# Nine gate/up pairs of the feed-forwards from three narrow matmuls per block to a wide and a narrow one

## The chip, the cores and the metric

The kernel runs on one core of a Trainium2 chip. The metric is the time of one execution on the device, in microseconds (us), as the median of several runs. Besides, one execution was recorded by the hardware profiler; its views (the page, groups of instructions, waits, the timeline) are quoted below. The engines are TensorE (PE; its weight loads are PEld), VectorE (DVE), ScalarE (ACT), GpSimd (POOL) and SyncE (SP), which issues the loads.

## The reference

One decoder layer on 512 tokens of width 1024: a feed-forward, a mixer (attention beside a recurrence), and a second feed-forward. Only the feed-forwards matter here, each of width 2816:

```
f = (silu(x @ w_gate) * (x @ w_up)) @ w_down
h = h + 0.5 * rms_norm(f, g)
```

Everything is float32.

## The kernel before, in words

**Two parts for each number.** TensorE multiplies a shortened float32. To keep the precision, each operand is split into a high part (the value rounded to the short form) and a low part (what is left). `split` does it: a copy on ScalarE writes the high part (L302), a subtraction on VectorE the low part (L303). A product then takes three matmuls for each block of 128 rows: high weights with the high input, high weights with the low input, low weights with the high input, all added up in one accumulator in PSUM.

**Seven products for eight.** The width 2816 is 22 tiles of 128 columns, numbered f = 0 to 21. The first few tiles of each feed-forward (six and three) are plain products. For each later tile the gate and the up projection are computed together as a *pair*: the contraction of 1024 is cut into two halves and the tokens into two halves of 256, and the 2 x 2 blocks of gate and up are obtained from seven products of sums of blocks (p1 to p7) instead of eight. `w_forms` makes the sums of the weights on VectorE and splits them; the sums of the input are made once. Each product runs over four row tiles of 128 (called blocks here), so a pair in the narrow form is 7 x 4 x 3 = 84 matmuls of 256 columns. The results come from chains: p1 is copied to a second accumulator, p6 and p7 go on adding to the first, and so on.

**The narrow form.** `seven_on` (L733) uses four accumulators of 256 columns. It runs p1, p5, p6, p2, p7, p3, p4 through `seventh` (L729 to L731 are its three matmuls). Between them ScalarE copies an accumulator to another or to SBUF (L743), always with higher priority. The gate's first half goes through Silu straight out of PSUM (L958), VectorE adds the second halves (L944 for the gate, which then goes through Silu at L945, L949 for up), and L954 multiplies gate and up, in two halves.

**The wide form.** `seven_wide` (L762) is in the kernel already, for the 16 pairs of the mixer. Its accumulators are whole PSUM banks of 512 columns, five of them. For each block one matmul of 512 columns (L779) multiplies the high weights with the high and the low input side by side, and one of 256 columns (L780) adds the low weights' product to the second half. So the two halves of a bank must be added when the chain ends: `fold` copies one half on ScalarE (L790) and adds the other on VectorE (L791); `sum_of` needs two adds on VectorE (L797, L798). `move` copies a bank of 512 columns to the next accumulator on ScalarE (L784).

**The down projection.** It is done in parts of four tiles, again by seven products, in four steps per part that are laid between the pairs: `ffn_order` writes the order of the events (weights of the next pair, weights of a down step, pair, down step) and `STEPS_AT` says which step follows which pair. In a step `down7` runs two or four groups of six matmuls of 512 columns (L1037 to L1039). Before a group, ScalarE writes the sum so far into its accumulator (the seed, L1026); after it, ScalarE copies it out (L1042). There are three such accumulators (`aux`), so the fourth group's seed waits for the first group's copy. `d_forms` makes the weights of a step. The tiles of the last part (f from 16 on) are split and wait for `last_product`, the plain product that ends a feed-forward.

**What sets the order.** Each engine runs its instructions in the order in which a scheduler has put them when the program is built; it goes by the order of the code and by priorities (`tc.high_priority`: weights ahead by 100, evictions of a pair by 200). Buffers come from pools: five accumulators `acc`, three `aux`, four weight tiles `w8` (1024 columns, both parts) and two `w4`, four raw weight buffers. So a weight tile for the next pair can only be split once an older one has been used, and a raw one can only be loaded once it has been split.

**At the pairs.** `prod` (L937) computes tile f. As `FIRST_ON` is 5, the narrow `seven_on` serves f = 6 to 21 of the first feed-forward and f = 5 to 21 of the second; f = 3 and 4 of the second use an older form, `seven`.

Of the kernel before, what the change touches and what calls it, by code (L numbers as in the profile page):

```python
# [20 lines left out]
NF = 22  # L21
FF_PARTS = ((0, 4), (4, 8), (8, 12), (12, 16), (16, 22))
NSTD = {1: 6, 2: 3}

SEVEN = range(4)
STEPS_AT = {1: ((6, 7, 7, 8), range(9, 13), range(13, 17), range(17, 21)),
# [4 lines left out]
HB = 256  # L31
# [3 lines left out]
FIRST_ON = {1: 5, 2: 5}  # L35
# [30 lines left out]
def ffn_order(n):  # L66

    order = [("std", f) for f in range(NSTD[n])]  # L70
    after = {}
# [3 lines left out]
    ready = False  # L75
    for f in range(NSTD[n], NF):
        if not ready:
# [106 lines left out]
def hybrid_layer(ctx: ExitStack, tc: tile.TileContext, xT: bass.AP, xN: bass.AP, wst: bass.AP,  # L184
# [120 lines left out]
    def acc_ps():  # L305
        return psum.tile([P, T], F32, name="acc", tag="acc", bufs=5)
# [4 lines left out]
    def tmp(name):  # L311
        return tpool.tile([P, T], F32, name=name, tag="t")
# [39 lines left out]
    HALVES = (slice(0, HB), slice(HB, T))  # L352
# [369 lines left out]
    def seventh(t, w, p, ps, start):  # L722
        at = t[p].at
        if len(at(0, 0).shape) == 3:
            ps = ps.rearrange("q (b t) -> q b t", b=2)
        for k in range(4):
            ks = slice(k * P, (k + 1) * P)
            wh, wl, xh, xl = w[p][:, 0, ks], w[p][:, 1, ks], at(0, k), at(1, k)
            PE.matmul(ps, wh, xh, start=start and k == 0, stop=False, skip_group_check=True)  # L729
            PE.matmul(ps, wh, xl, start=False, stop=False, skip_group_check=True)  # L730
            PE.matmul(ps, wl, xh, start=False, stop=k == 3, skip_group_check=True)  # L731

    def seven_on(t, w, g0, g1, u0, u1):  # L733

        b, z, y, v = (acc_ps()[:, :HB] for _ in range(4))

        def copy(ps, dst=None):
            if dst is None:  # L740
                dst = tpool.tile([P, HB], F32, name="c", tag="c", bufs=CB)
            with tc.high_priority(offset=EVAC):
                ACT.activation(dst, ps, AF.Copy)  # L743
            return dst

        seventh(t, w, "p1", b, True)
        copy(b, y)
        seventh(t, w, "p5", z, True)
        c5 = copy(z)
        seventh(t, w, "p6", b, False)  # L750
        c6 = copy(b)
        seventh(t, w, "p2", y, False)
        g0(y)
        seventh(t, w, "p7", b, False)
        copy(b, v)
        u1(b, c5)
        seventh(t, w, "p3", z, False)
        g1(z, c6)
        seventh(t, w, "p4", v, False)
        u0(v)  # L760

    def seven_wide(t, w, g, u, seen=lambda ap: ap, then=lambda: None):  # L762


        b, z, y, v, o = (acc_ps() for _ in range(5))

        def two(ps):
            return ps[:, :HB], ps[:, HB:]

        def product(p, ps, start):  # L770
            at = t[p].at
            part, cross = ps.rearrange("q (s c) -> q s c", s=2), two(ps)[1]
            if len(at(0, 0).shape) == 3:
                part = ps.rearrange("q (s b t) -> q s b t", s=2, b=2)
                cross = cross.rearrange("q (b t) -> q b t", b=2)
            for k in range(4):
                ks = slice(k * P, (k + 1) * P)
                wh, wl = w[p][:, 0, ks], w[p][:, 1, ks]
                PE.matmul(part, wh, at(BOTH, k), start=start and k == 0, stop=False, skip_group_check=True)  # L779
                PE.matmul(cross, wl, at(0, k), start=False, stop=k == 3, skip_group_check=True)  # L780

        def move(dst, src):
            with tc.high_priority(offset=EVAC):
                return ACT.activation(dst, src, AF.Copy).ins  # L784

        def fold(ps, dst=None):
            out = tpool.tile([P, HB], F32, name="c", tag="c", bufs=CB) if dst is None else dst
            x, y_ = two(ps) if dst is None else map(seen, two(ps))
            with tc.high_priority(offset=EVAC):
                ACT.activation(out, x, AF.Copy)  # L790
                DVE.tensor_add(out, y_, out)  # L791
            return out

        def sum_of(dst, ps, c):
            x, y_ = two(ps)
            with tc.high_priority(offset=EVAC):
                DVE.tensor_add(c, x, c)  # L797
                DVE.tensor_add(dst, seen(y_), seen(c))  # L798

        product("p1", b, True)  # L800
        move(y, b)
        product("p5", z, True)
        c5 = fold(z)
        product("p6", y, False)
        move(v, y)
        c6 = fold(y)
        product("p2", b, False)
        fold(b, g[0])
        product("p7", v, False)
        moved = move(o, v)  # L810
        sum_of(u[1], v, c5)
        with tc.issue_after(moved):
            then()
        product("p3", z, False)
        sum_of(g[1], z, c6)
        product("p4", o, False)
        fold(o, u[0])

    def seven(t, w, z, g, u):


        b, y = acc_ps()[:, :HB], acc_ps()[:, :HB]

        def product(p, ps, start):
            seventh(t, w, p, ps, start)

        def copy(ps):
            c = tpool.tile([P, HB], F32, name="c", tag="c", bufs=CB)
            with tc.high_priority(offset=EVAC):
                ACT.activation(c, ps, AF.Copy)  # L830
            return c

        def sum_of(dst, ps, c):
            with tc.high_priority(offset=EVAC):
                DVE.tensor_add(dst, ps, c)

        product("p1", b, True)
        c1 = copy(b)
        product("p2", y, True)
        sum_of(g[0], y, c1)  # L840
        product("p6", b, False)
        c6 = copy(b)
        product("p5", z, True)
        c5 = copy(z)
        product("p7", b, False)
        c7 = copy(b)
        sum_of(u[1], c7, c5)
        product("p4", y, True)
        sum_of(u[0], y, c7)
        product("p3", z, False)  # L850
        sum_of(g[1], z, c6)

    def ffn(n, x, r, forms_x, apool, pss):
        t, steps = forms_x
# [81 lines left out]

        def prod(f, w):  # L937
            g, u = tmp("g"), tmp("u")
            if f >= FIRST_ON[n]:
                lo, hi = HALVES  # L940

                def g1(z, c6):
                    with tc.high_priority(offset=EVAC):
                        DVE.tensor_add(g[:, hi], z, c6)  # L944
                    ACT.activation(g[:, hi], g[:, hi], AF.Silu)  # L945

                def u1(b, c5):
                    with tc.high_priority(offset=EVAC):
                        DVE.tensor_add(u[:, hi], b, c5)  # L949

                def u0(v):
                    def put(dst, view):
                        for q, (h, src) in enumerate(zip(HALVES, (v, u[:, hi]))):
                            DVE.scalar_tensor_tensor(dst[:, q] if len(dst.shape) == 3 else dst[:, h], g[:, h], -1.0,  # L954
                                                     src, op0=ALU.mult, op1=ALU.mult)
                    into(f, put)

                seven_on(t, w, lambda y: ACT.activation(g[:, lo], y, AF.Silu), g1, u0, u1)  # L958
                return
            seven(t, w, acc_ps()[:, :HB], [g[:, h] for h in HALVES], [u[:, h] for h in HALVES])  # L960
            ACT.activation(g, g, AF.Silu)
            into(f, lambda dst, v: DVE.scalar_tensor_tensor(dst, v(g), -1.0, v(u), op0=ALU.mult, op1=ALU.mult))

# [96 lines left out]

        keys = [(w, n, i) for i in range(NSTD[n]) for w in ("gate", "up")]
        forms = {}
        for ev in ffn_order(n):
            if ev[0] == "std":
                j = ev[1]
                while len(pss) < 2 * j + 2:
                    pss.append(acc_ps())
                    gemm(pss[-1], fetch(keys[len(pss) - 1]), x)
                with tc.high_priority(offset=EVAC if j == NSTD[n] - 1 else 0):
                    std_out(pss[2 * j], pss[2 * j + 1], j)  # L1070

                for step in steps[j:] if j == min(NSTD[n], 4) - 1 else steps[j:j + 1]:
                    step()
# [123 lines left out]
    with ExitStack() as mx:  # L1197
# [38 lines left out]
        def values_two(steps, then):  # L1236
# [78 lines left out]
            for j in range(2):  # L1315
# [4 lines left out]
        t, steps = forms_of(lambda i, j: Form(lambda s, k: um_t[2 * i + k // 2][:, s, k % 2, HALVES[j]]),  # L1320
                            apool, False, rec_half)
# [167 lines left out]
        for c in range(0, KC, 2):  # L1489
            g, u = tmp("g"), tmp("u")  # L1490
# [12 lines left out]
    with ExitStack() as mx:  # L1503
# [146 lines left out]
        for i, (what, hd) in enumerate(LRU_ORDER):  # L1650
# [9 lines left out]
            def then():  # L1660
                if i + 1 < len(LRU_ORDER):
                    prepare(LRU_ORDER[i + 1])
# [21 lines left out]
        for c in range(KC):  # L1684
            if c < 3:
                ps = pss[c]
            else:
# [17 lines left out]
                 {(1, 3): lambda: (bd2.turn(0), bd2.turn(1))})  # L1705
    keys = [(w, 2, i) for i in range(NSTD[2]) for w in ("gate", "up")]
    pss = gemm_first(keys[:NFIRST], u2, [spare(ap2)["tx"]],
# [144 lines left out]
```

## Time and profile before

| | |
|---|---|
| median of 3 runs | 1212.2 us (1211.42 to 1212.27) |
| the profiled execution | 1211.87 us |
| its span, first to last instruction | 1210.1 us |
| first feed-forward's pairs, f = 6 to 21 | about 72 to 310 us |
| mixer's wide pairs | about 407 to 600 us |
| second feed-forward's pairs, f = 3 to 21 | about 900 to 1171 us |

In a row of the groups stand line, engine, operation, tile written and tiles read, shape and count, then the busy time in us and the mean of one in ns, then the idle time of the engine just before them and what ended it. In a timeline row stand the start and the duration in us. A row of the waits names who waited for whom, with total us, times and longest. A row of the stretches gives the length, and the busy time of each engine asked for, in the order PE, PEld, DVE, ACT, POOL, then the granted clock.

### The profile page before, as it was taken

What the parts mean: (1) busy time and instruction counts of PE and PEld (TensorE: products, weight loads), DVE (VectorE), ACT (ScalarE), POOL (GpSimd) and SP (SyncE); (2) the same over time, 40 slices, a digit from 0 to 9 for tenths busy, and PEclk for the clock granted to TensorE, in tenths of its full rate; (3) what the DMA queues carried; (4) which work ended last, traced back from release to release, by engine and by line L of the source; (5) the groups of instructions that cost most, each with busy time, mean ns of one, the idle gap of its engine ahead of it and who ended that gap; (6) DMA issues with size and microseconds to landing.
All of it is one profiled execution on the core that took longest, in us unless ns stands there. A gap on an engine that the chain in (4) does not pass through costs nothing.

```text
span 1210.1 us, 18990 instructions
## 1 busy us (share of the span) xinstructions
PE 1199.2 (99%) x7306; PEld 1073.7 (89%) x7306; DVE 1029.0 (85%) x1608; ACT 832.4 (69%) x1447; POOL 26.1 (2%) x51
## 2 busy tenths in 40 slices
PE   9999999999999999999999999999999999999997
PEld 8899999999888889888889888888899999999996
DVE  7999888989689899999867899775799888888964
ACT  7566787887566576677735897834566687877763
POOL 0000000000011000000000000000100000000000
PEclk9999999999999999999999999999999999999999
DMA  7234343435625232222323432235443333343341
GB/s 266 87 97 140 114 138 116 133 118 157 243 109 145 70 114 79 88 96 70 126 77 111 145 135 87 87 110 186 148 137 117 123 121 125 121 130 115 123 174 70
DMA packets 45819, 149.78 MB, mean 124 GB/s; under 512 B 5152, under 2 KB 8608, under 8 KB 45728
## 3 DMA queue, kind: packets, MB, share of 16 engines
q1 hardware_dynamic: 38160, 131.09, 32.5%
q0 software_dynamic: 7280, 17.30, 4.2%
q8 instruction: 57, 0.93, 0.3%
q14 instruction: 34, 0.28, 0.1%
q10 hardware_dynamic: 288, 0.17, 0.0%
HBM read 138.06 MB, written 6.29 MB: 119 GB/s over the span
## 4 chain that ended last, share of the span: by engine, by line
PE 88%; DVE 6%; ACT 3%; DMA 2%; issue 1%; DVEq 0%
PE acc L729 9%; PE acc L731 9%; PE acc L730 9%; PE acc L779 8%; PE acc L315 7%; PE acc L317 7%; PE acc L316 7%; PE acc L780 4%; PE aux L1037 3%; PE aux L1038 3%; PE aux L1039 3%; DVE w L303 2%; DMA raw<-in_w 2%; PE acc L433 2%; PE acc L432 2%; PE acc L431 2%
## 5 line engine op out<-in xcount | busy, mean ns | idle before, releaser
L303 DVE TENSOR_TENSOR w<-raw,w 128x1024 fp32r<-128x1024 f32 (+1 forms) x272 | 297.4, 1098 | 36.2 <-ACT w L302 35.2
L302 ACT ACTIVATE w<-raw 128x1024 fp32r<-128x1024 f32 (+1 forms) x272 | 259.9, 959 | 89.4 <-PE acc L317 42.7
L729 PE MATMUL acc<-big,w 128*128 128x256 f32 x920 | 260.5, 283 | 0.0
L731 PE MATMUL acc<-big,w 128*128 128x256 f32 x920 | 260.3, 283 | 0.0
L730 PE MATMUL acc<-big,w 128*128 128x256 f32 x920 | 260.3, 283 | 0.0
L729 PEld LDWEIGHTS acc<-big,w 128*128 128x128 f32 x920 | 176.2, 192 | 1.9
L730 PEld LDWEIGHTS acc<-big,w 128*128 128x128 f32 x920 | 176.2, 192 | 1.7
L731 PEld LDWEIGHTS acc<-big,w 128*128 128x128 f32 x920 | 176.3, 192 | 0.0
L779 PE MATMUL acc<-big,w 128*128 128x512 f32 x320 | 115.0, 397 | 0.0
L780 PE MATMUL acc<-big,w 128*128 128x256 f32 x320 | 90.8, 284 | 0.0
L1037 PE MATMUL aux<-w,xf 128*128 128x512 f32 x224 | 87.5, 393 | 1.4 <-ACT w L302 0.9
L1038 PE MATMUL aux<-w,xf 128*128 128x512 f32 x224 | 87.5, 391 | 0.0
L1039 PE MATMUL aux<-w,xf 128*128 128x512 f32 x224 | 87.2, 389 | 0.0
L779 PEld LDWEIGHTS acc<-big,w 128*128 128x128 f32 x320 | 60.1, 188 | 13.2 <-ACT acc L784 0.2
L303 DVE TENSOR_TENSOR w<-s,w 128x1024 fp32r<-128x1024 f32 x51 | 62.2, 1220 | 3.2 <-ACT w L302 2.7
L780 PEld LDWEIGHTS acc<-big,w 128*128 128x128 f32 x320 | 60.4, 189 | 0.1
L315 PE MATMUL acc<-xf,w 128*128 128x512 f32 (+1 forms) x168 | 58.8, 352 | 0.0
L316 PE MATMUL acc<-xf,w 128*128 128x512 f32 (+1 forms) x168 | 58.6, 349 | 0.0
L317 PE MATMUL acc<-xf,w 128*128 128x512 f32 (+1 forms) x168 | 58.6, 349 | 0.0
L302 ACT ACTIVATE w<-s 128x1024 fp32r<-128x1024 f32 x51 | 53.9, 1057 | 6.2 <-PE acc L731 3.0
L743 ACT ACTIVATE c<-acc 128x256 f32<-128x256 f32 x74 | 28.2, 383 | 40.4 <-PE acc L731 40.2
L1037 PEld LDWEIGHTS aux<-w,xf 128*128 128x128 f32 x224 | 41.9, 188 | 10.2 <-ACT w L302 1.5
(453 smaller groups left out, 2934.2 us busy)
## 6 DMA issues: line engine op xcount, KB each, us to landing
raw<-in_w SPq DMA_DIRECT2D x232, 512.0 KB, 3.5
big<-xf POOLq DMA_DIRECT2D x6, 512.0 KB, 3.4
gains<-in_rows POOLq DMA_DIRECT2D x5, 512.0 KB, 5.4
h<-in_x SPq DMA_DIRECT2D x8, 256.0 KB, 5.3
h<-in_xn POOLq DMA_DIRECT2D x4, 512.0 KB, 6.0
kept_m<-h POOLq DMA_DIRECT2D x4, 512.0 KB, 2.9
vals<-in_w SPq DMA_DIRECT2D x4, 512.0 KB, 6.2
h<-kept_m POOLq DMA_DIRECT2D x4, 512.0 KB, 6.1
```

The lines of the kernel that those rows point to most:

```text
L302: state["split"] = ACT.activation(dh, src, AF.Copy).ins
L303: state["low"] = DVE.tensor_sub(dl, src, dh.bitcast(F32)).ins
L315: PE.matmul(ps, wh, xh, start=first, stop=False)
L316: PE.matmul(ps, wh, xl, start=False, stop=False)
L317: PE.matmul(ps, wl, xh, start=False, stop=last)
L729: PE.matmul(ps, wh, xh, start=start and k == 0, stop=False, skip_group_check=True)
L730: PE.matmul(ps, wh, xl, start=False, stop=False, skip_group_check=True)
L731: PE.matmul(ps, wl, xh, start=False, stop=k == 3, skip_group_check=True)
L779: PE.matmul(part, wh, at(BOTH, k), start=start and k == 0, stop=False, skip_group_check=True)
L780: PE.matmul(cross, wl, at(0, k), start=False, stop=k == 3, skip_group_check=True)
L1037: PE.matmul(ps, xh, wh, start=first and j == 0, stop=False, skip_group_check=True)
L1038: PE.matmul(ps, xh, wl, start=False, stop=False, skip_group_check=True)
```

## The change

A table names nine tiles, four of the first feed-forward and five of the second, and `prod` hands these to `seven_wide` instead of `seven_on`. Gate and up come out as whole tiles in SBUF, so the code behind the branch, which until now served only the older form, does the Silu over 512 columns and one product over 512 columns. The computation is the same. In the first feed-forward the tiles 10, 14 and 18 have a down step of four groups behind them, and so have 9, 13 and 17 in the second; behind tile 20 of the second comes tile 21, and behind tile 21 of either the last product.

```diff
+WIDE = {1: (10, 14, 18, 21), 2: (9, 13, 17, 20, 21)}
...
         def prod(f, w):
             g, u = tmp("g"), tmp("u")
-            if f >= FIRST_ON[n]:
+            if f in WIDE[n]:
+                seven_wide(t, w, *([x[:, h] for h in HALVES] for x in (g, u)))
+            elif f >= FIRST_ON[n]:
                 lo, hi = HALVES
...
                 seven_on(t, w, lambda y: ACT.activation(g[:, lo], y, AF.Silu), g1, u0, u1)
                 return
-            seven(t, w, acc_ps()[:, :HB], [g[:, h] for h in HALVES], [u[:, h] for h in HALVES])
+            else:
+                seven(t, w, acc_ps()[:, :HB], [g[:, h] for h in HALVES], [u[:, h] for h in HALVES])
             ACT.activation(g, g, AF.Silu)
             into(f, lambda dst, v: DVE.scalar_tensor_tensor(dst, v(g), -1.0, v(u), op0=ALU.mult, op1=ALU.mult))
```

The function that is now called, cut to its core:

```python
def seven_wide(t, w, g, u, seen=lambda ap: ap, then=lambda: None):
    b, z, y, v, o = (acc_ps() for _ in range(5))
...
        for k in range(4):
...
            PE.matmul(part, wh, at(BOTH, k), start=start and k == 0, stop=False, skip_group_check=True)
            PE.matmul(cross, wl, at(0, k), start=False, stop=k == 3, skip_group_check=True)
...
    product("p1", b, True)
    move(y, b)
    product("p5", z, True)
    c5 = fold(z)
    product("p6", y, False)
    move(v, y)
    c6 = fold(y)
    product("p2", b, False)
    fold(b, g[0])
    product("p7", v, False)
    moved = move(o, v)
    sum_of(u[1], v, c5)
...
    product("p3", z, False)
    sum_of(g[1], z, c6)
    product("p4", o, False)
    fold(o, u[0])
```

All line numbers are those of the kernel before, as in its profile.

## The prediction

> **What bounds the kernel now.** The page comes first: its busy table says which engine fills the span, its slices whether the clock was granted, and its groups what a matmul costs in either form.
>
> ```profile
> span 1210.1 us, 18990 instructions
> ...
> PE 1199.2 (99%) x7306; PEld 1073.7 (89%) x7306; DVE 1029.0 (85%) x1608; ACT 832.4 (69%) x1447; POOL 26.1 (2%) x51
> ...
> PEclk9999999999999999999999999999999999999999
> ```
>
> TensorE is busy 99% of 1210.1 us at full clock; VectorE (85%) and ScalarE (69%) are behind it. So time falls only where TensorE's own stream gets shorter, and rises where another engine makes it wait. The waits of TensorE in the second feed-forward (895 to 1192 us) show how little waiting there is to win:
>
> ```profile
> PE aux L1037 <- ACT w L302: 0.9, 3, 0.5
> PE aux L1037 <- ACT aux L1026: 0.5, 1, 0.5
> ```
>
> In the first one (60 to 320 us) this view has no row at all: the 16 pairs and their down steps there run without a gap.
>
> A matmul's duration in the groups overlaps the next one's, so I read prices from starts. The timeline of TensorE, from the first matmul of one pair to the first of what follows: narrow pair 10 of the first feed-forward, then three stretches of 28 wide blocks of the mixer (one block is the matmuls of one of the four row tiles of a product) that ran without a wait.
>
> ```profile
> 136.73 0.28 PE L729 MATMUL acc<-big,w 128*128 128x256 f32 x1
> ...
> 146.81 0.40 PE L1037 MATMUL aux<-w,xf 128*128 128x512 f32 x1
> ...
> 407.01 0.39 PE L779 MATMUL acc<-big,w 128*128 128x512 f32 x1
> ...
> 416.89 0.39 PE L779 MATMUL acc<-big,w 128*128 128x512 f32 x1
> ...
> 455.08 0.39 PE L779 MATMUL acc<-big,w 128*128 128x512 f32 x1
> ...
> 464.86 0.39 PE L779 MATMUL acc<-big,w 128*128 128x512 f32 x1
> ...
> 489.15 0.39 PE L779 MATMUL acc<-big,w 128*128 128x512 f32 x1
> ...
> 498.89 0.39 PE L779 MATMUL acc<-big,w 128*128 128x512 f32 x1
> ```
>
> Narrow: 146.81 - 136.73 = 10.08 us for 84 matmuls, 0.36 per block of three. Wide: 9.88, 9.78 and 9.74 us for 56 matmuls, 0.353 to 0.348 per block of two. Both forms stream the same 768 columns per block; a pair differs by 0.20 to 0.34 us, not by a third.
>
> **The change, part by part.** *The pace.* At nine pairs 84 matmuls become 56 (-252 in all). Saving between 9 x 0.20 = 1.8 and 9 x 0.34 = 3.1 us. I take the middle one of the three stretches, 0.30 a pair, 2.7 us.
>
> [...]
>
> *The evictions.* Prices from the mixer, where the wide form runs already (405 to 602 us), beside the narrow form's (60 to 320 us):
>
> ```profile
> L784 ACT ACTIVATE acc<-acc 128x512 f32<-128x512 f32 x48 | 28.3, 589 | 11.0 <-PE acc L780 8.4 <-DVE e L1437 1.1 <-DVE xch L1415 1.1
> L790 ACT ACTIVATE c<-acc 128x256 f32<-128x256 f32 x32 | 12.1, 379 | 9.1 <-PE acc L780 8.9
> L791 DVE TENSOR_TENSOR c<-acc,c 128x256 f32<-128x256 f32 x32 | 13.4, 420 | 4.0 <-ACT c L790 3.9
> L743 ACT ACTIVATE c<-acc 128x256 f32<-128x256 f32 x32 | 12.1, 382 | 14.2 <-PE acc L731 14.1
> L949 DVE TENSOR_TENSOR u<-acc,c 128x256 f32<-128x256 f32 x16 | 6.7, 418 | 0.0
> L303 DVE TENSOR_TENSOR xf<-tt,xf 128x512 fp32r<-128x512 f32 x12 | 8.1, 686 | 0.0
> ```
>
> A pair on ScalarE: four copies and two half Silus (6 x 0.38 = 2.3 us) become three moves of 0.59, four copies of 0.38 and one Silu of 512 columns (about 0.6, as the move): 3.9 us, so +1.6. On VectorE: two adds and two half products (4 x 0.42 = 1.7) become eight adds of 0.42 and one product of 512 columns (0.69, as the last row): 4.1 us, so +2.4. Whether that is hidden is read from busy times of the stretches of pair 10 with its down step, and of pair 20 of the second feed-forward, which has no down step behind it:
>
> ```profile
> 136.73:152.27 15.54, 15.54 (x109) 1.00 0.39 123
> ...
> 136.70:152.20 15.50, 15.50 (x109) 14.54 (x108) 12.53 (x17) 12.01 (x23) 0.00 (x0) 1.00 0.38 121
> ...
> 1150.50:1160.60 10.10, 10.10 (x86) 10.06 (x85) 8.06 (x11) 7.62 (x15) 0.00 (x0) 1.00 0.43 144
> ```
>
> Pair 10: VectorE (third busy time) has 3.0 us idle, ScalarE (fourth) 3.5; both additions fit. Pair 20: VectorE has 2.0 idle against 2.4, short by 0.4. What covers that is the lead of the weights: the low half for product p5 of pair 11 is split at 148.21 and used at 153.71.
>
> ```profile
> 148.21 1.23 DVE L303 TENSOR_TENSOR w<-s,w 128x1024 fp32r<-128x1024 f32 x1 [0.17 <-ACT w L302]
> ...
> 153.71 0.28 PE L729 MATMUL acc<-big,w 128*128 128x256 f32 x1
> ```
>
> That is 153.71 - 149.44 = 4.3 us of cover. So I cost both additions at nothing, in eight pairs; if the cover went, each would cost up to its overrun.
>
> *Waits added.* The instruction order of the changed program puts the two adds of u's and g's second half and the fold of u's first half in one block on VectorE, behind p4's end; next in its queue are the splits of the following pair's weights (p1/p2, p5/p6). Behind pair 10 that moves the p5/p6 split back by about 0.5 us, out of 4.3. On ScalarE the last fold waits for p4's end, and behind it stand a weight split, the Silu, the first eviction of the down step (L1042), in some pairs one more split, and then the seed (L1026) that the fourth group of the down step needs. Counted from the pair's start: p4's results at 9.95, fold 0.3, split 0.95, Silu, eviction and split 0.5 each, seed 0.6, done at 13.3; the fourth group starts at 9.77 + 3 x 1.36 = 13.85 (a group is a quarter of 15.54 - 10.08). 0.55 us are left. In pair 10 today the seed ends at 149.81 and the fourth group starts at 146.81 + 4.08 = 150.89, 1.1 later:
>
> ```profile
> 149.21 0.60 ACT L1026 ACTIVATE aux<-ea 128x512 f32<-128x512 f32 x1
> ```
>
> Cost nothing, but this is the thinnest cover. Moves between chains (p1 to p6, p6 to p7, p7 to p4) end 0.3 us or more ahead of use; in pair 20 the third ends 0.1 late. That is 0.1 on the sum.
>
> *TensorE's order.* Outside the nine pairs it changes in three places, and these have a price. In the first feed-forward the first matmuls of two groups of the fourth down step move up between p1 and p5 of pairs 12 and 16. They use weights whose buffer comes free only when the previous down step ends, so ScalarE must evict and split while p1 runs. The second feed-forward has that order already, and shows what it costs:
>
> ```profile
> 1014.30 0.59 ACT L1042 ACTIVATE ea<-aux 128x512 f32<-128x512 f32 x1
> 1014.78 1.05 ACT L302 ACTIVATE w<-raw 128x1024 fp32r<-128x1024 f32 x1
> ...
> 942.26 0.28 PE L731 MATMUL acc<-big,w 128*128 128x256 f32 x1
> 943.00 0.73 PE L1037 MATMUL aux<-w,xf 128*128 128x512 f32 x2 [0.46 <-ACT w L302]
> ...
> 1015.40 0.28 PE L731 MATMUL acc<-big,w 128*128 128x256 f32 x1
> 1015.88 0.73 PE L1037 MATMUL aux<-w,xf 128*128 128x512 f32 x2 [0.20 <-ACT w L302]
> 1016.45 0.28 PE L729 MATMUL acc<-big,w 128*128 128x256 f32 x1
> ```
>
> 1015.40 to 1016.45 is 1.05 us for work of 0.12 + 2 x 0.23 = 0.58: 0.47 lost. At 942.26 the wait is 0.26 longer: 0.73. Two new places: between 0 and 1.5, I take 2 x 0.47 = 0.9, since ScalarE's order there is now that of 1014.30.
>
> At pair 21 of the second feed-forward two early matmuls of the last product stand behind p1 instead of one. Their weights were split just in time:
>
> ```profile
> 1160.84 1.06 ACT L302 ACTIVATE w<-raw 128x1024 fp32r<-128x1024 f32 x1 [0.20 <-PE acc L731]
> ...
> 1162.08 0.40 PE L431 MATMUL aux<-w,act 128*128 128x512 f32 x1
> ```
>
> Ready at 1161.90, used at 1162.08. Now the last fold of pair 20 (0.30) goes first and p1 is shorter by 0.05, so it is 0.17 late, 0.3 with the restart of about 0.1 seen above. Bounds 0 and 0.5; I take 0.3.
>
> *A stall that may go.* Pair 17 of the second feed-forward, which is made wide, carries the largest wait of its stage:
>
> ```profile
> 1114.23 1.22 DVE L989 TENSOR_TENSOR raw<-raw 128x1024 f32<-128x1024 f32 x1 [1.24 <-DMA raw<-in_w]
> ...
> 1119.56 0.62 ACT L302 ACTIVATE act<-u 128x512 fp32r<-128x512 f32 x1
> 1120.08 0.59 ACT L1026 ACTIVATE aux<-ea 128x512 f32<-128x512 f32 x1
> ...
> 1119.84 0.39 PE L1039 MATMUL aux<-w,xf 128*128 128x512 f32 x1
> 1120.72 0.50 PE L1037 MATMUL aux<-w,xf 128*128 128x512 f32 x1 [0.49 <-ACT aux L1026]
> 1121.05 0.39 PE L1038 MATMUL aux<-w,xf 128*128 128x512 f32 x1
> ```
>
> A late load holds VectorE at 1114.23, so the product of pair 17 is late, ScalarE's split of it (1119.56) too, and the seed behind that. 1119.84 to 1121.05 is 1.21 us for 2 x 0.23: 0.76 lost. In the new order the add that needs the load stands behind the pair's sums, and the seed ahead of that split. Between 0 and -0.76; I take all of it.
>
> Loads keep their order on SP's queue and POOL's. *The sum*, on the profiled execution (1211.87 us): -2.7 + 0.1 + 0.9 + 0.3 - 0.8 = -2.2, so 1209.7. That execution lies 0.3 below the median of the runs, 1212.2; against the median I forecast 1212.2 - 2.2 = 1210.0.
>
> **The rivals.** *The early matmuls cost nothing new*, because the stream reaches pairs 12 and 16 otherwise than at 1014 us. Without 0.9 and 0.3 the time is 1212.2 - 3.4 = 1208.8. For it: the first feed-forward has no such wait today. Against: the order there becomes that of the second. *The pace gives little* (1.8), the early matmuls cost their upper 1.5, pair 17's stall stays: -1.8 + 0.1 + 1.5 + 0.3 = +0.1, 1212.3, no change. For it: 942.26 shows the higher price, and the first wide stretch the lower gain; against: the two other wide stretches, and a seed that no longer stands behind the late split. [...] *Slower: the seed comes late.* Its cover is the 0.55 us above; from there on the fourth group of the down step waits. Pair 17's stall is that mechanism, at 0.76. At the six other wide pairs with a down step behind them, and with pair 17's kept: -2.7 + 0.1 + 0.9 + 0.3 + 6 x 0.76 = +3.2, 1215.4. For it: two engines, each with more work in order, meet there; against: the sum of ScalarE's queue above. That the change does not do what it says can be left out: the program's order has the 252 matmuls fewer.
>
> **How the numbers follow.** Forecast 0.50, no new cost 0.22, little pace 0.10, late seed 0.18. A measurement of this kernel can tell about 0.2% from no change, 2.4 us: below 1209.8 is faster, above 1214.6 slower. The forecast's own range is 1208.3 (3.1 + 0.8 saved, nothing lost) to 1212.4 (1.8 saved, 1.5 + 0.5 lost); 0.21 of its 0.50 lies below 1209.8. Faster: 0.21 + 0.22 = 0.43. Slower: the late seed where most places show it, 0.13. Same: 0.44. The range reaches from 1208.2 over the first two rivals and a late seed at up to half the places, to 1213.8.
>
> **What would show it.** In the profile after: 28 blocks of 0.348 to 0.353 us at each of the nine places; waits of L1037 on L302 at pairs 12 and 16 of the first feed-forward (a new row), near 0.2 us plus restart; no wait on L1026 at pair 17; about 0.3 us behind p1 of pair 21. The prediction is wrong if waits on L1026, or on weight splits by VectorE, appear at several wide pairs, or if a wide block takes 0.36.

## The result and the profile after

Changed kernel: 1214.93 us (median of 10 runs) against 1212.24 us in the same job. Ratio 1.0025, 95% interval 1.0017 to 1.0033: slower by 2.7 us, outside the forecast range, which ended at 1213.8. The profiled execution took 1214.97 us, with a span of 1213.2.

The page of the changed kernel has fewer matmuls, the same clock and a longer span:

```profile
span 1213.2 us, 18602 instructions
...
PE 1199.6 (99%) x7054; PEld 1061.1 (87%) x7054; DVE 1045.0 (86%) x1653; ACT 842.8 (69%) x1465; POOL 26.1 (2%) x51
...
PEclk9999999999999999999999999999999999999999
```

252 matmuls are gone. VectorE has 16 us more and ScalarE 10, which is 1.8 and 1.2 us for each of the nine pairs. TensorE's waits, as the view of waits gives them for the first feed-forward (60 to 322 us; before it had no row) and then the second (895 to 1195 us; columns: total, times, longest):

```profile
PE aux L1041 <- ACT w L303: 1.2, 2, 0.6
...
PE aux L1041 <- ACT w L303: 2.1, 3, 1.2
PE aux L1041 <- ACT aux L1030: 0.4, 1, 0.4
```

L1041 is L1037 of before, L303 is L302, L1030 is L1026. Where the time went, read pair by pair from the starts on TensorE in the two profiled executions (a pair counts with what stands behind it, up to the start of the next):

| place | us |
|---|---|
| ahead of the first wide pair (the same code) | +0.5 |
| pace of seven wide pairs, 0.20 each | -1.4 |
| pairs 20 and 21 of the second feed-forward (+0.07, +0.15) | +0.2 |
| new early matmuls, pairs 12 and 16 of the first (+0.92, +0.86) | +1.8 |
| pair 17 of the second | -0.8 |
| second: pairs 10 and 11 (+0.09, +0.94), pair 15 (+0.48) | +1.5 |
| first: ahead of pair 21 (+0.39); second: pair 19 and ahead of 20 (+0.27, +0.73) | +1.4 |
| pair 6 of the second, mixer, last product (no change there) | -0.2 |
| sum, before rounding | +3.1 |

Pair 21 of the second took 10.69 us, 0.38 more than before, but it holds one matmul of the last product more, which is 0.23 of work moved and not lost.

The pace is small but there. Pair 10 of the first feed-forward, from its first matmul to the down step behind it:

```profile
137.25 0.39 PE L780 MATMUL acc<-big,w 128*128 128x512 f32 x1
...
147.13 0.40 PE L1041 MATMUL aux<-w,xf 128*128 128x512 f32 x1
```

9.88 us against 10.08, 0.353 per block. The new early matmuls of pair 12 stand behind p1, whose last matmul is the first row:

```profile
166.73 0.28 PE L732 MATMUL acc<-big,w 128*128 128x256 f32 x1
167.59 0.73 PE L1041 MATMUL aux<-w,xf 128*128 128x512 f32 x2 [0.58 <-ACT w L303]
168.16 0.28 PE L730 MATMUL acc<-big,w 128*128 128x256 f32 x1
```

1.43 us for 0.58 of work: 0.85 lost, not 0.47 (the rest of the 0.92 is lost later in the pair). And the same place in pair 11 of the second, where 0.47 was lost before, loses 2.00 - 0.58 = 1.42:

```profile
1017.01 0.28 PE L732 MATMUL acc<-big,w 128*128 128x256 f32 x1
1018.45 0.73 PE L1041 MATMUL aux<-w,xf 128*128 128x512 f32 x2 [1.15 <-ACT w L303]
1019.01 0.28 PE L730 MATMUL acc<-big,w 128*128 128x256 f32 x1
```

Pair 11 is narrow in both kernels. What comes late there starts on another queue. These are the issues on SyncE's queue of the load behind pair 10 of the first feed-forward and behind pairs 9 and 17 of the second, before and then after:

```profile
150.06 0.33 SPq L242 DMA_DIRECT2D raw<-in_w  x1
...
999.17 0.33 SPq L242 DMA_DIRECT2D raw<-in_w  x1
...
1115.48 0.33 SPq L242 DMA_DIRECT2D raw<-in_w  x1
```

```profile
153.74 0.33 SPq L243 DMA_DIRECT2D raw<-in_w  x1
...
1004.39 0.33 SPq L243 DMA_DIRECT2D raw<-in_w  x1
...
1122.63 0.33 SPq L243 DMA_DIRECT2D raw<-in_w  x1
```

TensorE is 0.5, 1.7 and 2.9 us later at these pairs than before; the loads are 3.7, 5.2 and 7.2 later. So each is 3.2 to 4.3 us late against its own pair. Behind pairs 14 and 18 of the first and 13 of the second, the one that is delayed most is 3.2, 5.6 and 5.4 us late. A load waits for one of four raw buffers, which VectorE frees as it ends the last split that reads one. Before, behind pair 10, that was the 512-column split:

```profile
149.35 0.69 DVE L303 TENSOR_TENSOR w<-raw,w 128x512 fp32r<-128x512 f32 x1
149.95 0.69 DVE L691 TENSOR_TENSOR s<-raw 128x512 f32<-128x512 f32 x1
151.33 1.23 DVE L303 TENSOR_TENSOR w<-raw,w 128x1024 fp32r<-128x1024 f32 x1 [0.70 <-ACT w L302]
153.54 0.69 DVE L692 TENSOR_TENSOR s<-s,raw 128x512 f32<-128x512 f32 x1 [0.98 <-DMA raw<-in_w]
```

It ends at 150.04, and the load goes out at 150.06. After, on VectorE:

```profile
147.43 0.41 DVE L799 TENSOR_TENSOR u<-acc,c 128x256 f32<-128x256 f32 x1
147.76 0.41 DVE L799 TENSOR_TENSOR g<-acc,c 128x256 f32<-128x256 f32 x1
148.09 0.41 DVE L792 TENSOR_TENSOR u<-acc,u 128x256 f32<-128x256 f32 x1
...
151.29 0.68 DVE L692 TENSOR_TENSOR s<-raw 128x512 f32<-128x512 f32 x1
151.90 0.68 DVE L966 SCALAR_TENSOR_TENSOR tt<-g,u 128x512 f32<-128x512 f32 x1
152.50 1.82 DVE L304 TENSOR_TENSOR w<-raw,w 128x1024 fp32r<-128x1024 f32 x2
...
157.65 0.69 DVE L693 TENSOR_TENSOR s<-s,raw 128x512 f32<-128x512 f32 x1 [1.00 <-DMA raw<-in_w]
```

The 512-column split is now the second of the two at 152.50, behind the adds, the product and a 1024-column split; that one is the first to free a buffer, at 152.50 + 1.22 = 153.72, and the load goes out at 153.74. The adds are not all of it: the new order also puts the sum at 151.29 and the 1024-column split ahead, which stood behind the 512-column split before (149.95 and 151.33). VectorE waits 1.00 us for that load at 157.65, 20.4 us behind the start of pair 10. Before, it waited 0.98 at 153.54, 16.8 us behind it. So the wait is no longer than it was, but everything behind it in VectorE's queue is 3.6 us later.

The loads behind a late one go out closer together. Behind pair 9 of the second feed-forward three went out from 999.17 to 1005.13 us before, and from 1004.39 to 1006.73 after. Their median time from issue to landing rose from 3.5 to 5.3 us; no run shows whether that is because they stand closer together.

In pair 11 of the second feed-forward the lateness reaches ScalarE; before, and then after:

```profile
1010.07 0.63 ACT L302 ACTIVATE w<-raw 128x512 fp32r<-128x512 f32 x1 [1.04 <-DVE raw L696]
```

```profile
1013.93 0.63 ACT L303 ACTIVATE w<-raw 128x512 fp32r<-128x512 f32 x1 [2.64 <-DVE raw L697]
...
1016.87 0.58 ACT L1046 ACTIVATE ea<-aux 128x512 f32<-128x512 f32 x1
1017.35 1.05 ACT L303 ACTIVATE w<-raw 128x1024 fp32r<-128x1024 f32 x1
```

Behind the late split stand the evictions, and behind these the split at 1017.35 for which TensorE waits until 1018.45.

The third loss is in ScalarE's order. Ahead of the last wide pairs one seed of the down step, which stood ahead of the step, now stands behind its first eviction. In pair 19, ScalarE before, then ScalarE and TensorE after:

```profile
1142.24 0.59 ACT L1026 ACTIVATE aux<-facc 128x512 f32<-128x512 f32 x1
```

```profile
1149.43 0.58 ACT L1046 ACTIVATE facc<-aux 128x512 f32<-128x512 f32 x1
1149.91 1.11 ACT L1030 ACTIVATE aux<-facc 128x512 f32<-128x512 f32 x2
```

```profile
1149.77 0.39 PE L1043 MATMUL aux<-w,xf 128*128 128x512 f32 x1
1150.55 0.50 PE L1041 MATMUL aux<-w,xf 128*128 128x512 f32 x1 [0.40 <-ACT aux L1030]
```

### The profile page after: what moved, and what is told of

Same layout as the page of the kernel before. It is cut to its first block, busy times and chain, and to the rows that moved or that the text cites. A ratio compares the mean times of both kernels' runs of the same rounds, so it can differ in the third digit from the quotient of the medians.

```text
span 1213.2 us, 18602 instructions
## 1 busy us (share of the span) xinstructions
PE 1199.6 (99%) x7054; PEld 1061.1 (87%) x7054; DVE 1045.0 (86%) x1653; ACT 842.8 (69%) x1465; POOL 26.1 (2%) x51
## 4 chain that ended last, share of the span: by engine, by line
PE 84%; DVE 8%; ACT 3%; DMA 2%; issue 2%; DVEq 0%; ACTq 0%
PE acc L780 12%; PE acc L316 7%; PE acc L318 7%; PE acc L317 7%; PE acc L730 6%; PE acc L781 6%; PE acc L732 6%; PE acc L731 6%; DVE w L304 3%; PE aux L1041 3%; PE aux L1042 3%; PE aux L1043 3%; DMA raw<-in_w 2%; PE acc L434 2%; PE acc L432 2%
## 5 line engine op out<-in xcount | busy, mean ns | idle before, releaser
L303 ACT ACTIVATE w<-raw 128x1024 fp32r<-128x1024 f32 (+1 forms) x272 | 259.9, 960 | 84.2 <-PE acc L318 45.4
L730 PE MATMUL acc<-big,w 128*128 128x256 f32 x704 | 199.5, 283 | 0.0
L732 PE MATMUL acc<-big,w 128*128 128x256 f32 x704 | 199.2, 283 | 0.0
L731 PE MATMUL acc<-big,w 128*128 128x256 f32 x704 | 199.1, 283 | 0.0
L780 PE MATMUL acc<-big,w 128*128 128x512 f32 x536 | 192.3, 398 | 0.0
L781 PE MATMUL acc<-big,w 128*128 128x256 f32 x536 | 151.4, 282 | 0.0
L730 PEld LDWEIGHTS acc<-big,w 128*128 128x128 f32 x704 | 134.8, 192 | 1.9 <-ACT acc L744 0.2
L731 PEld LDWEIGHTS acc<-big,w 128*128 128x128 f32 x704 | 134.8, 192 | 1.5
L732 PEld LDWEIGHTS acc<-big,w 128*128 128x128 f32 x704 | 134.8, 192 | 0.0
L780 PEld LDWEIGHTS acc<-big,w 128*128 128x128 f32 x536 | 100.7, 188 | 23.6 <-ACT acc L785 0.6
L781 PEld LDWEIGHTS acc<-big,w 128*128 128x128 f32 x536 | 101.2, 189 | 0.5
L1041 PE MATMUL aux<-w,xf 128*128 128x512 f32 x224 | 87.5, 394 | 3.7 <-ACT w L303 3.2
L303 ACT ACTIVATE w<-s 128x1024 fp32r<-128x1024 f32 x51 | 53.8, 1055 | 5.7 <-PE acc L732 3.0
L785 ACT ACTIVATE acc<-acc 128x512 f32<-128x512 f32 x75 | 44.4, 592 | 18.3 <-PE acc L781 14.5
L1041 PEld LDWEIGHTS aux<-w,xf 128*128 128x128 f32 x224 | 41.7, 188 | 13.5 <-ACT w L303 4.2
```

Of the source, the lines that this page charges most:

```text
L303: state["split"] = ACT.activation(dh, src, AF.Copy).ins
L1041: PE.matmul(ps, xh, wh, start=first and j == 0, stop=False, skip_group_check=True)
```

## The experiments

Theory A: the wide form's adds stand ahead of the split that frees a raw buffer; loads go out late, all preparation behind them is late, and early matmuls are where TensorE meets that. Rivals: B, only TensorE's order and ScalarE's added work count; C, the lateness moves on if the early matmuls go; D, VectorE's amount of work counts, not its order. The kernel before ran with each job, 1211.8 to 1212.1 us; ratios are to it, with 95% intervals. The intervals reach about 1 us to either side, so smaller differences between kernels are read from one profiled execution of each and hold for that execution.

**The hold.** Each down step is queued on TensorE behind the last matmul of the pair ahead of it (kept in `state["mm"]` by `seventh` and `product`), in the changed kernel and in the kernel before.

```diff
-                down7(*ev[1:], forms.pop(ev[1:]))
+                with tc.issue_after(state["mm"]):
+                    down7(*ev[1:], forms.pop(ev[1:]))
```

> The changed kernel, with every down step's matmuls held behind the last matmul of the pair ahead of it on TensorE, so that none stands between p1 and p5 any more. Theory A (late buffers): behind a wide pair VectorE frees a raw weight buffer 3 to 5 us later, the next load and all weight preparation behind it come late, and the early matmuls are where TensorE meets that. Then the waits inside pairs 12 and 16 of the first feed-forward (0.92 and 0.86) and inside 6, 11 and 15 of the second (0.47, 1.42, 0.96) go, and what is left are the waits in front of pair 20, at 19 and in 21: 1214.9 - 4.6 = 1210.3, with the loads still late. Rival C (the lateness just moves on): the same weights are then late for p5 or for the down step itself, and the time stays at 1213 or more.

> The kernel before with the same hold on the down steps, no pair changed. If the early matmuls are a price of their own, the waits of 0.73, 0.47 and 0.47 us in pairs 6, 11 and 15 of the second feed-forward go, and perhaps the 0.17 each behind them: 1212.2 - 1.7 to 2.2 = 1210.0 to 1210.5. Rival C: the time stays at 1212. The difference to the changed kernel with the same hold is what the wide form is worth without early matmuls: by theory A about nothing (-1.3 pace, -0.8 at pair 17, +2.0 of late weights elsewhere).

Measured: kernel before with the hold 1210.36 (0.9989, 0.998 to 0.9997), changed kernel with it 1211.56 (0.9999, 0.9991 to 1.0008). The first is as expected: its waits in pairs 6, 11 and 15 are gone, and the early matmuls have a price of their own even without the change. The second lies between A (1210.3) and C: 3.4 us gained, and new waits where the late weights now hold ScalarE's copies, 0.77 and 0.57 us in pairs 12 and 16 of the first feed-forward. Pair 19 of the second loses 1.25. The two kernels with the hold differ by 1.2 us, where A gave about nothing. In the changed kernel with the hold, the waits there:

```profile
PE acc L730 <- ACT c L744: 0.8, 2, 0.5
```

The load behind pair 10 goes out at 153.28, 2.9 us late against its pair. So the early matmuls are where much of the lateness shows, not what makes it.

**The adds behind the splits.** In the nine pairs `fold` and `sum_of` add at ordinary priority:

```diff
         def sum_of(dst, ps, c):
             x, y_ = two(ps)
-            with tc.high_priority(offset=EVAC):
+            with tc.high_priority(offset=0 if cut else EVAC):
                 DVE.tensor_add(c, x, c)
```

`cut` is true in the nine pairs; the add in `fold` is treated in the same way.

> The changed kernel with the halves' adds on VectorE in the nine pairs at ordinary priority, so that in its queue the weight splits of the next pair, above all the 512-column one that frees a raw buffer, stand ahead of them. The early matmuls in pairs 12 and 16 of the first feed-forward go away by this too, those of the second stay. Theory A: the loads behind wide pairs go out within 1 us of where they did before, and the extra waits of the second feed-forward (0.94 at pair 11, 0.48 at 15, 1.0 at 19) and the 0.39 of the first go as well: 1214.9 - 1.8 - 2.8 = 1210.3. Rival B (only TensorE's order and ScalarE's added work count, loads don't): the 1.8 alone goes, 1213.1.

Measured: 1211.60 (0.9998, 0.999 to 1.0007), halfway between A and B. The three loads:

```profile
150.56 0.33 SPq L243 DMA_DIRECT2D raw<-in_w  x1
...
998.26 0.33 SPq L243 DMA_DIRECT2D raw<-in_w  x1
...
1113.91 0.33 SPq L243 DMA_DIRECT2D raw<-in_w  x1
```

Against their pairs they are 0.3 us late twice and then early. The extra of pair 15 is gone, that of pair 11 falls from 0.94 to 0.44, pair 19 with the gap behind it from 1.0 to 0.41. What stays is the late seed (0.41 twice), and late adds cost something new, 0.14 and 0.32 in pairs 10 and 14. Of the 2.9 us of extra waits in the table (its lines of +1.5 and +1.4), 1.2 are gone: A holds for that part. The other 1.7 stays though these three loads are on time; ahead of pair 11 a later one is 1.3 us late again. The 1.8 of pairs 12 and 16 of the first feed-forward is gone too, but the early matmuls left these pairs with the same edit, so it can't be put down to the loads.

**Fewer adds.** `fold` in the nine pairs without its add, so that half of gate and up is left out; the freeing split stays where it is.

> The changed kernel without the four adds of the folds in each of the nine pairs (half of gate and up is left out), 1.3 us less of VectorE a pair; the 512-column split stays behind the product in VectorE's queue. The early matmuls in pairs 12 and 16 of the first feed-forward go away by this too. Theory A: loads behind wide pairs still 2 to 3 us late, so half or more of the second feed-forward's extra waits stays: 1214.9 - 1.8 - (0 to 1.4) = 1211.7 to 1213.1. Rival D (VectorE's amount of work, not its order): all of them go, 1210.3.

Measured: 1212.14 (1.0004, 0.9994 to 1.0013), in A's range and not near D's 1210.3: the load behind pair 10 is still 2.5 us late, and pairs 11 and 15 of the second feed-forward keep their extra (0.88, 0.48). Pair 19 and the seeds lose nothing. But pair 12 of the first feed-forward loses 0.63 at a copy of ScalarE, though no early matmul stands there any more, and pair 20 of the second 0.46.

**Five raw buffers.** Both kernels with the ring of raw buffers one longer; `CB = 4` and three temporary tiles make the room.

> The changed kernel with five raw weight buffers in place of four; room is made by four small buffers for the copied halves in place of six and three temporary tiles in place of four. To be read against its twin without the wide pairs, whose matmul order is the same around pairs 12 and 16, so that the early matmuls there don't count. Theory A (late buffers): with a buffer more, loads behind wide pairs don't go out later than in the twin by more than 1 us, and the nine pairs are worth their pace, -1.7, with no extra wait at 11, 15 and 19: twin - 1.7. Rival B (more work on ScalarE and VectorE delays the weights whatever the loads do): the extra of 0.9 + 0.5 + 1.0 + 0.4 us stays: twin + 1.1.

> The twin: the kernel before with the same buffers (five raw, four for copied halves, three temporary). The scheduler then puts early matmuls into pairs 12 and 16 of the first feed-forward, as the change did: if such a place costs 0.5 to 0.9 us by itself, this is 1 to 1.8 above 1212 less what loads on time save: 1211.5 to 1213.5. If early matmuls cost nothing once loads are early, about 1211.

Measured: 1221.69 (1217.0 to 1223.8) and 1222.34 (1220.2 to 1223.3). With the smaller rings the part between the two feed-forwards alone takes 4.0 and 6.0 us more than before, so the totals decide nothing. The stage does: from the start of pair 9 of the second feed-forward to that of pair 21, in the twin and then in the wide one (the middle row is the issue of the load behind pair 9):

```profile
994.28 0.28 PE L729 MATMUL acc<-big,w 128*128 128x256 f32 x1
...
1006.70 0.33 SPq L242 DMA_DIRECT2D raw<-in_w  x1
...
1170.88 0.28 PE L729 MATMUL acc<-big,w 128*128 128x256 f32 x1
```

```profile
990.73 0.39 PE L780 MATMUL acc<-big,w 128*128 128x512 f32 x1
...
1005.54 0.33 SPq L243 DMA_DIRECT2D raw<-in_w  x1
...
1165.65 0.39 PE L780 MATMUL acc<-big,w 128*128 128x512 f32 x1
```

176.60 and 174.92: the wide kernel is 1.7 us shorter there. Its pace gives 0.6 (pairs 9, 13 and 17). Waits that only the twin has, in pairs 11, 12 and 18 (0.40, 0.87, 0.45), give 1.7. Waits that only the wide kernel has take 0.6 back: 0.42 in pair 9's own down step, where a seed comes late, and 0.17 in pair 10. With four buffers it is 1.2 longer in the same stretch (985.73 to 1160.64 before, 987.44 to 1163.58 after).

Pairs 11, 15 and 19 show no extra over the twin, as A has it. A's other sign fails: loads behind the wide pairs still go out late, by (1005.54 - 990.73) - (1006.70 - 994.28) = 2.4 us behind pair 9 and by 0.8 to 1.9 behind the other five with a down step, where A allowed 1. And 1.7 us of waits that only the twin has show how much a change of rings moves by itself. So the fifth buffer shortens the lateness and takes these extras away; it does not show that the loads were all of it. The twin also prices the early matmuls alone, pair 12 of the first feed-forward:

```profile
168.46 0.28 PE L731 MATMUL acc<-big,w 128*128 128x256 f32 x1
168.95 0.72 PE L1037 MATMUL aux<-w,xf 128*128 128x512 f32 x2 [0.21 <-ACT w L302]
169.51 0.28 PE L729 MATMUL acc<-big,w 128*128 128x256 f32 x1
```

1.05 - 0.58 = 0.47, the price of the forecast; what the change showed above that (0.85 in all) goes with the lateness.

**One wide pair.** `WIDE = {1: (10,), 2: ()}` in the changed kernel.

> The changed kernel with pair 10 of the first feed-forward alone made wide. By theory: -0.19 for its pace, the load behind it 3 to 4 us late, 0.92 less 0.0 in pair 12 of which 0.46 is the early matmuls and 0.46 the lateness, and everything behind as in the kernel before: 1211.9 + 0.7 = 1212.6, with pairs 14 to 21 unchanged. If the lateness builds up over several wide pairs, pair 12 loses only the 0.46.

Measured: 1212.76 (1.0008, 0.9999 to 1.0017). The median fits by luck, the parts don't: the load behind pair 10 is 3.1 us late, yet pair 12 loses only 0.46. With the pace that makes +0.3, and the median is 1.0 above the kernel before. The profiled execution took 1214.50, the slowest of ten, with 3.35 us lost in pair 15 of the second feed-forward, where nothing was changed (last section); whether the others hold some of that is not known. With the same order on the engines up to there the full change lost 0.9. There the load landed at 157.56, 20.3 us behind the start of pair 10; with one wide pair at 156.67, 19.9 behind. So in these two executions a few tenths in a landing time go with a late load that costs nothing and one that costs half a microsecond.

**Both edits and beyond.** Hold and late adds together; then also the Silu and product of the nine pairs at the eviction priority; then pairs 20 and 21 of the second feed-forward narrow again; and, in place of these two, hold and adds at the preparation's priority (100).

> Both edits in one: the changed kernel with its adds at ordinary priority and with the down steps held behind the pair ahead. If the two prices add up (late buffers and early matmuls are two causes), the loads are on time, the waits inside pairs 6, 11 and 15 of the second feed-forward go as they did in the kernel before with the hold (-1.6 there), and 0.4 each in front of the last wide pairs stays: 1211.6 - 1.6 = 1210.0, and down to 1209.2 if the 0.4 and 0.3 extra of pairs 11 and 14 go too. If they are one cause (a late VectorE shows wherever TensorE stands closest), the hold brings nothing more: 1211.5.

> The kernel with the hold and the adds at ordinary priority, and with the Silu and the product of the nine pairs at the eviction priority, so that ScalarE's copies for TensorE don't stand behind a split that waits for a late product; the order also puts the seeds of the last down step back to where they are in the kernel before. Theory: the waits on ScalarE's copies in pair 12 of the first feed-forward (0.24) and pairs 10 and 14 of the second (0.96, 0.52) and those on seeds ahead of the last wide pairs (0.44, 0.41) go; what is left over the unchanged kernel with the hold is pace, -0.19 at seven places, and 0.46 lost in pairs 20 and 21: 1210.4 - 1.3 + 0.5 = 1209.6. If ScalarE is simply too full there, the waits stay and the time is 1210.6 again.

> The same with pairs 20 and 21 of the second feed-forward narrow again. The 0.46 lost there (two early matmuls of the last product, late moves) goes too: 1210.4 - 0.19 x 7 = 1209.0. If these two pairs had cost nothing, the same as the kernel above.

> The kernel with the hold and the adds at the priority of the weight preparation, between the two settings so far: in VectorE's queue the buffer-freeing split of 512 columns stands ahead of the last four adds and the product ahead of the sums that wait for the next load. Theory: loads on time (within 1 us), no waits on ScalarE's copies in pairs 10 and 14 of the second feed-forward; the seeds of the last down step are in their late place, so 0.4 to 0.8 each stays ahead of the last wide pairs, and 0.46 in 20 and 21: 1210.4 - 1.3 + 0.5 + 1.0 = 1210.6.

Measured: 1210.64 (0.999, 0.9981 to 0.9998), 1211.76 (0.9999, 0.999 to 1.0007), 1213.70 (1.0012, 1.0003 to 1.002) and 1210.77 (0.9994, 0.9985 to 1.0003). The first comes out 0.6 above its sum; in its profiled execution (1211.83) the extra waits move to ScalarE's copies in pairs 10 and 14 of the second feed-forward (0.96, 0.52). The product's priority was to free those copies and did not: such waits appear in more pairs (0.26 to 0.77; 1.4 in two of them in the third kernel, 4.7 above its expectation). Why narrow pairs 20 and 21 make the earlier ones worse stays open. The fourth has no such wait in pairs 10 and 14 and meets its forecast in the total, not in its terms: pair 20 of the first feed-forward and pair 19 of the second lose 1.3 and 1.4, half of it inside the pair and half at the seeds behind it, against 0.4 to 0.8 each in the sum. Five raw buffers on top of the first two edits took 1222.84 and, for the rings, tell nothing.

**The work without the form, and the form without its costs.** First the kernel before with six unused adds behind each of the nine narrow pairs; then hold, adds at priority 100 and `WIDE = {1: (10, 14, 21), 2: (9, 13)}`.

> The kernel before, all pairs narrow, with six more adds of 256 columns on VectorE behind each of the nine pairs (2.0 us of work a pair; their result is not used), about what the wide form adds there. In VectorE's queue the buffer-freeing split stays ahead of most of them, and TensorE's order is that of the kernel before. Theory A (the place of the split counts): loads behind the nine pairs at most 1 to 1.5 us later than before, and 0 to 0.8 us in all: 1211.8 to 1212.6. Rival D (the amount of VectorE's work counts): the extra waits of the change outside the early matmuls, 0.94, 0.48, 1.0 and 0.4, come back without the wide form: 1214.6.

> The kernel with the hold and the adds at the priority of the weight preparation, with only pairs 10, 14 and 21 of the first feed-forward and 9 and 13 of the second wide. The seeds of the last down steps are back in their early place, the loads are on time, and no early matmul stands inside a pair. If these three were all of the cause, the wide form is left with its pace: the unchanged kernel with the hold, less 5 x 0.19: 1210.4 - 1.0 = 1209.4, and no wait on seeds ahead of the last pair. If a wide pair has a price of its own, 1210.4 or more.

Measured: 1213.95 (1.0016, 1.0007 to 1.0025) and 1210.11 (0.9984, 0.9975 to 0.9993). The first is nearer to D. In the first feed-forward loads stay on time and nothing is lost up to pair 20; 0.6 go behind pair 21, where the last product waits for VectorE. In the second the loads behind the nine pairs are at most 0.5 us late against their pairs, and 0.25, 0.66, 0.43 and 0.34 are lost at pairs 10, 11, 18 and 19. These are only in part the places that D named: pair 15 loses nothing. The loss of pair 11 goes with a load behind pair 9 that took 4.6 us to land (3.5 before); VectorE waits 1.57 us for it at 1004.88, and the next but one goes out 1.6 us late. So VectorE's added work costs without the form, too, though not place by place as in the change. The second kernel beats both the kernel before and the changed one, but its gain is the hold's: the kernel before with the hold alone took 1210.36, and the difference is within the intervals. Its wide pairs save 5 x 0.20 and lose 0.51 and 0.79 again in pairs 10 and 14, behind pairs 9 and 13:

```profile
PE acc L730 <- ACT acc L744: 0.7, 2, 0.4
```

## Why the prediction was wrong

- **The step that failed** is "Loads keep their order on SP's queue and POOL's" together with "I cost both additions at nothing, in eight pairs". The order was kept; the times were not. The cover was measured as the lead of a weight over TensorE, 4.3 us, and behind pair 10 it held: after the change that split ends at 150.78 and is used at 154.03, 3.25 us later (forecast 3.8). The same queue on VectorE also frees raw buffers, and there was no cover: the load went out 0.02 us after the split ended. The work that VectorE got more, ahead of that split, and the new order of its queue became loads that go out 3.2 to 5.6 us late. The extra of pairs 10, 11, 15, 19 and ahead of the last wide pairs, 2.9 us, had no term in the sum. Five buffers take the extra of pairs 11, 15 and 19 away; adds behind the splits take 1.2 of the 2.9.
- **The account of the miss.** Forecast -2.2 and measured +3.1 on the profiled executions differ by 5.3 us: 2.9 for the extra waits without a term, 0.9 for the early matmuls, 0.7 for the pace of seven pairs, 0.4 for pairs 20 and 21, the rest mostly where nothing was changed.
- **The added work.** Forecast 2.4 us a pair on VectorE and 1.6 on ScalarE, measured 1.8 and 1.2. The forecast added up durations, but neighbours overlap: the adds at 147.43, 147.76 and 148.09 last 0.41 and start 0.33 apart. So the added work was even less than forecast, and still not free.
- **Pace.** Forecast 0.30 a pair, measured 0.20, the lower bound, in seven pairs; in the two that follow each other without a down step, waits inside them (0.25 and 0.34) take more than the pace gives. The first of the three wide stretches (9.88) was the one that held. 10.08 us for 84 matmuls and 9.88 for 56 are 0.20 for 28 matmuls fewer; no run shows what each of these carries.
- **Early matmuls in pairs 12 and 16.** The place was right and the price alone too (0.47, measured 0.47 in the twin and 0.46 with one wide pair); with late loads it was 0.92 and 0.86, above the dearer price of 0.73 that the prediction had read at 942.26.
- **Pairs 20 and 21 of the second feed-forward.** 0.1 and 0.3 were forecast beside the pace of 0.6: -0.2. Measured +0.2: the pace is 0.4, pair 20 loses 0.25 at its moves (10.13 against 9.88), and pair 21 loses 0.34 at its early matmuls, near the forecast of 0.3.
- **Pair 17.** The stall went, -0.8 as forecast, but by luck as far as the runs show. In the kernel before with the hold and in the one with one wide pair, pair 17 is narrow and the stall is gone as well (-0.77, -0.79). It goes with the time that one load takes from issue to landing, the one that goes out at 1109.40 before: 4.7 us in the kernel before and 5.1 in the one with unused adds, which have the stall, 3.7 and 3.4 in the two without it, and 3.5 in the changed kernel. No run shows what the wide form does to the stall when the load is slow.
- **The late seed** gave 1215.4, near the measured time, for another reason. At the wide pairs' own down steps the cover of 0.55 held in the changed kernel: in pair 10 the seed is done at 150.37, 13.1 us from the start of the pair, against 13.3 forecast. Late seeds cost 0.4 to 0.7 at two other places, where the scheduler had moved them.
- **The range.** It ended 1.1 us below the measured time: it was made from the bounds of the terms and from late seeds, and the 2.9 us were no term.

How the remaining extra divides between the place of the freeing split and VectorE's amount of work is not settled: with the split late and 1.3 us less work a pair the extra of pairs 11 and 15 stays (0.88, 0.48); with the split in time and 2.0 us of unused work a pair 1.9 us are lost, partly at other places.

## What to carry to other kernels

An engine that prepares data frees buffers too: for work added ahead of it, look at how soon after its last reader the next load goes out. Where that is at once (0.02 us here), there is no cover, whatever lead the data has over its user (3.25 us behind pair 10). A change in one stage can then be paid for a pair or two later (here 0.94 us in pair 11, behind the wide pair 9), at the place where the busiest engine stands closest to its data; such a place can be worth as much as the change's own gain: the hold took 1.6 us off the kernel before, the pace 1.4 off the changed one.

## What the runs showed of the hardware

In the kernel with one wide pair a load of the second feed-forward took 5.4 us from issue to landing where it took 3.5 before (VectorE, which waited for it, went on at 1070.75 us, before at 1068.84), and in pair 15 TensorE stood still from 1075.6 to 1077.9 us for what hung on it. The table of stretches there (columns: length, busy time and count of PE, PEld, DVE, ACT and POOL, granted clock, DMA share, GB/s):

```profile
1075.50:1077.90 2.40, 0.30 (x4) 0.10 (x2) 1.00 (x1) 2.37 (x5) 0.00 (x0) 0.97 0.69 239
1077.90:1079.20 1.30, 1.30 (x4) 1.11 (x5) 1.27 (x2) 0.68 (x2) 0.00 (x0) 0.50 0.84 303
1079.20:1080.40 1.20, 1.20 (x8) 1.20 (x8) 1.16 (x2) 0.00 (x0) 0.00 (x0) 0.50 0.11 44
1080.40:1081.20 0.80, 0.80 (x5) 0.80 (x5) 0.00 (x0) 0.00 (x0) 0.00 (x0) 0.53 0.59 159
1081.20:1082.50 1.30, 1.30 (x13) 1.30 (x12) 0.00 (x0) 0.38 (x1) 0.00 (x0) 1.00 0.75 290
```

Behind that wait the granted clock was 0.50 to 0.53 for 3.3 us: the two early matmuls at 1077.87 took 1.22 us, those at 1075.96 in the kernel before 0.73. The load was 1.9 us late, and 3.35 us were lost in the pair. Behind the wait of 1017.01 in the changed kernel, 1.3 us long, the clock stayed at 1.00. It is one event in one execution; no run shows how long a wait must be for the clock to fall.
